# The second half's norm marked into the next product, and eight sums of squares made one, in a two-layer hybrid backbone

## The chip, the cores and the metric

The kernel runs on one core of one Trainium2 chip. The metric is the device time of one execution, in microseconds. Three runs of the kernel before stand behind its median.

## The reference, cut to what matters

A trunk of two layers works on 256 context tokens and 256 latent tokens of 1,024 channels, in float32. Each layer has three sub-layers: a half-step SwiGLU, a mixer (retention, a gated linear recurrence and attention, merged and projected), and a second half-step SwiGLU. Each of them begins with the same normalisation, and this is what the change touches:

```python
def _rms(x, g):
    xf = x.astype(jnp.float32)
    y = xf * lax.rsqrt(jnp.mean(xf * xf, axis=-1, keepdims=True) + NORM_EPS)
    return (y * g.astype(jnp.float32)).astype(x.dtype)

def _modulate(x, g, shift, scale):
    return _rms(x, g) * (1 + scale) + shift
...
x = x + m_l[:, 0..2] * sublayer(_modulate(x, norm_g, shift, scale))
```

Here `shift`, `scale` and the gate `m[:, 2]` are computed from the conditioning vectors, one set for context and one for latent tokens.

## The kernel before

**Layout.** The residual `x` stands in SBUF as eight tiles `x[d]` of 128 channels by 512 tokens: columns 0 to 255 are the context, 256 to 511 the latent tokens. The modulated input of a sub-layer is kept as two float32r tiles for each `d`, `hh[d]` (the rounded value) and `hl[d]` (the rest), and each weight likewise as `wh` and `wl`; a product is three matmuls, `wh*hh`, `wl*hh` and `wh*hl` (`mm3`, lines 145 to 147).

**The border between two sub-layers.** The last product of a sub-layer makes the eight output tiles of 128 channels one after the other. Six of them are made for all 512 tokens at once. The last two, `d` = 6 and 7, are made in `finish` in two halves: first columns 0 to 255 of both (tile `pl`), then columns 256 to 511 of both. A half is 72 matmuls of 256 columns behind a SwiGLU (two tiles of 12 contraction steps of three matmuls) and 48 behind the mixer of layer 0 (two tiles of 8 steps).

**What follows each half.** `update` adds the gated product to `x[d]` on VectorE (line 596), then `sumsq` squares it on ScalarE (line 585) and adds the square to `st["acc"]` on VectorE (line 587); the square of the last tile, `d` = 7, is not added but kept as `st["last"]`. `token_ms` lets TensorE sum over the channels: for each 128 tokens one matmul with `acc` and one with `last` as the weights and a single column of ones, into `ssq` (line 621). In float32 each of these is two instructions, so a half has eight. `rstd_bcast` makes the reciprocal root on VectorE (ten small instructions, `rv` and lines 161 to 169, then `dg`, line 609) and spreads it over the partitions with one matmul into `rb` (line 611). `modulate` then makes, for each of the eight `d`, `hn` on VectorE (line 641), `hh` on ScalarE (line 642) and `hl` on VectorE (line 643).

**The next product.** `proj_first` makes the first four tiles (`lx` ahead of the mixer, `pa` and `pb` ahead of a SwiGLU) with weights loaded ahead by `preload`. It goes by halves as well: for columns 0 to 255 first 64 matmuls with `hh` (item by item, for each of eight `k` the weights `wh` and `wl`, line 739), then 32 with `hl` (line 736); then the same 96 for columns 256 to 511.

**Where these stand.** `finish` runs with 512 tokens at four borders: layer 0 first SwiGLU to mixer, mixer to second SwiGLU, second SwiGLU to layer 1 first SwiGLU, and that to the mixer of layer 1. At the fifth border, inside layer 1, only latent tokens remain, and `finish_ahead` has an order of its own, written out by hand. `token_ms` is so called nine times.

**What sets the order.** Outside of the parts under `manual_schedule` a planner writes the order of each engine's instructions ahead of time: it follows the program on its own estimates of durations and gives each engine what it holds to be ready. The chip then runs each engine's list strictly in the order written. `issue_after(ins)` is a constraint on that order: what the block traces on the engine of `ins` is placed behind `ins`. `finish` uses it in this way: `marks` holds pairs of a count and an instruction, and a matmul step of the half that follows is held behind the instruction once the count is reached. With `MA, MB = 4, 13` the steps of the second half from number 4 on (12 matmuls) stand behind the first half's `ssq`, and those from number 13 on (39 matmuls) behind its `rb`. For the second half's own norm there is no such mark in the next product.

`hold` is the last `modulate` of the second half; weight splits (`wload`) and the background products of the conditioning (`pump`) that are traced after it are held behind it in the same way.

Of the kernel before, what the change touches and what calls it, by code (L numbers as in the profile page):

```python
# [16 lines left out]
P = 128  # L17
D = 1024
KD = D // P
# [15 lines left out]
SW = 128  # L35


MA, MB = 4, 13
NA, NB = 2, 4

LAG = 3
# [26 lines left out]
class Net:  # L68
# [509 lines left out]
    def sumsq(self, d, st, c0, c1):  # L578

        nc = self.nc  # L580
        sq = st["sq"][d] if d in st.setdefault("sq", {}) else self.tmp("sq")
        st["sq"][d] = sq
        if d == 0:
            st["acc"] = sq
        nc.scalar.activation(sq[:, c0:c1], self.x[d][:, c0:c1], AF.Square)
        if 0 < d < KD - 1:
            nc.vector.tensor_tensor(st["acc"][:, c0:c1], st["acc"][:, c0:c1], sq[:, c0:c1], op=ALU.add)
        if d == KD - 1:
            st["last"] = sq

    def update(self, d, ps, tab, c0, c1, st, nlo):

# [22 lines left out]
    def token_ms(self, st, c):  # L615

        nc = self.nc
        sp = self.sm_ps("ssq", [P, 2])
        for t in range(2):
            for n in ("acc", "last"):  # L620
                mm = nc.tensor.matmul(sp[:, t:t + 1], lhsT=st[n][:, c + t * P:c + (t + 1) * P],
                                      rhs=self.ones[:, 0:1], start=n == "acc", stop=n == "last")
        self.last_pe = mm.ins
        v = self.tiny("rv", [P, 2])
        nc.vector.tensor_scalar(v, sp, 1.0 / D, EPS, op0=ALU.mult, op1=ALU.add)
        return v
# [19 lines left out]
    def finish(self, tiles, tab, lo, st, nxt):  # L646


        nlo = nxt["lo"] if nxt else CTX
        if nxt:  # L650
            self.drain(nxt["tab"])
            self.h_tiles()
        ps = {d: self.mm_ps("pl") for d, _ in tiles}
        marks = []
        for c, v in self.halves(lo):
            n = 0
            for d, mms in tiles:
                for mm in mms(ps[d], c, c + 256):
                    with ExitStack() as es:
                        for at, ins in marks:  # L660
                            if n >= at:
                                es.enter_context(self.tc.issue_after(ins))
                        mm()
                    n += 1
                self.update(d, ps[d], tab, c, c + 256, st, nlo)
            if nxt and c >= nlo:
                v2 = self.token_ms(st, c)
                marks = [(MA, self.last_pe)]
                r = self.rstd_bcast(v2)
                marks += [(MB, self.last_pe)]  # L670
                self.hold = [self.modulate(d, r, nxt["tab"], c, v) for d in range(KD)][-1]

    def ahead_tiles(self, nxt):

        self.drain(nxt["tab"])
        self.xs = []
        for i in range(0, 2 * KD, 6):
            n = min(6, 2 * KD - i)
            t = self.big("xs", F32R, [P, n, TOK - CTX + 2])
            self.xs += [t[:, k] for k in range(n)]  # L680
            self.split(t[:, 0::2, 0:2], t[:, 1::2, 0:2], nxt["tab"]["Bt"][:, i // 2:(i + n) // 2])
# [45 lines left out]
    def proj_first(self, lo):  # L727

        pss = [self.mm_ps(name) for _, name in self.pre]
        mm = self.nc.tensor.matmul  # L730
        for sl in [slice(c, c + 256) for c, _ in self.halves(lo)]:
            for i in range(2):
                for ((wh, wl), _), ps in zip(self.pre, pss):
                    for k in range(KD):
                        if i:
                            mm(ps[:, sl], lhsT=wh[:, k], rhs=self.hl[k][:, sl], start=False, stop=k == KD - 1)
                            continue
                        for w in (wh, wl):
                            mm(ps[:, sl], lhsT=w[:, k], rhs=self.hh[k][:, sl], start=k == 0 and w is wh, stop=False)
        return pss  # L740
# [704 lines left out]
```

## Time and profile before

| what | value |
|---|---|
| median of three runs | 2136.7 us (2136.7 to 2139.08) |
| the profiled execution, its own time | 2137.75 us |
| its span, first to last instruction | 2135.9 us |
| mean granted TensorE clock | 0.999 |
| TensorE busy | 2099.5 us, 98% of the span |
| VectorE busy | 1526.1 us, 71% |
| ScalarE busy | 877.9 us, 41% |
| GpSimd busy | 29.2 us, 1% |

A busy TensorE isn't a TensorE at its peak: matmuls overlap, and their ends are modelled. What a matmul costs in a full stream is read from the distance of two starts, not from its duration. An idle engine that is not the one that sets the end costs nothing; here that engine is TensorE nearly everywhere, so that a change is worth what it does to the distances between TensorE's starts.

### The profile page before, as it was taken

Reading aid. Unit: us, or ns where it says so; the run is one execution under the profiler, and the core shown is the slowest. Engines: PE = TensorE matmul, PEld = TensorE weight load, DVE = VectorE, ACT = ScalarE, POOL = GpSimd, SP = SyncE. Lnnn points to the kernel's source line nnn. Section 1 sums busy time; section 2 is a strip of 40 time slices with the busy share of each in tenths; the row PEclk is TensorE's granted clock in tenths of the full one; section 3 lists DMA queues with packets and bytes.
Section 4 is the critical chain, followed back from the end, with each engine's and each line's share of the span. In section 5 each row is a group of like instructions: output and inputs, shape, how many; then the busy total and the mean of one; then the engine's idle time right before and its main releaser. Section 6 shows DMA issues by size and latency. Waiting matters only on the chain. (4 is left out here: it accounts for less than half of the span.)

```text
span 2135.9 us, 29550 instructions
## 1 busy us (share of the span) xinstructions
PE 2099.5 (98%) x11301; PEld 1788.5 (84%) x11301; DVE 1526.1 (71%) x2858; ACT 877.9 (41%) x1379; POOL 29.2 (1%) x48
## 2 busy tenths in 40 slices
PE   8999999999999999999999999999999999999998
PEld 5788888988878777988788898888889899989996
DVE  6998988675574866766766778777666777877555
ACT  4422323387323564332223332222233674665443
POOL 0000000100000000000000000000000000000001
PEclk9999999999999999999999999999999999999999
DMA  8566666332223314254654625465552435555663
GB/s 274 173 178 199 196 185 186 104 97 81 84 79 89 90 40 123 76 158 134 179 159 131 184 84 158 141 183 154 148 164 64 119 113 150 148 150 164 182 177 128
DMA packets 424239, 300.63 MB, mean 141 GB/s; under 512 B 11517, under 2 KB 372562, under 8 KB 424096
## 3 DMA queue, kind: packets, MB, share of 16 engines
q1 hardware_dynamic: 421120, 294.17, 47.0%
q0 software_dynamic: 1472, 3.42, 0.6%
q8 instruction: 89, 1.46, 0.3%
q10 hardware_dynamic: 1504, 1.13, 0.2%
q14 instruction: 54, 0.44, 0.1%
HBM read 297.64 MB, written 1.05 MB: 140 GB/s over the span
## 5 line engine op out<-in xcount | busy, mean ns | idle before, releaser
L132 ACT CAST wh<-raw 128x1024 fp32r<-128x1024 f32 (+3 forms) x437 | 412.5, 947 | 849.2 <-issue 187.3
L133 DVE TENSOR_TENSOR wl<-raw,wh 128x1024 fp32r<-128x1024 f32 (+3 forms) x437 | 476.0, 1092 | 248.2 <-ACT wh L132 244.3
L539 DVE SCALAR_TENSOR_TENSOR macc<-mraw,s_col,macc 128x512 f32<-128x512 f32 x448 | 315.9, 749 | 41.3 <-DMA mraw<-in_w_mod_dram 41.2
L145 PE MATMUL pb<-hh,wh 128*128 128x512 f32 (+1 forms) x656 | 238.8, 364 | 0.2 <-ACT wh L132 0.2
L147 PE MATMUL pb<-hh,wl 128*128 128x512 f32 (+1 forms) x656 | 238.6, 364 | 0.0
L146 PE MATMUL pb<-hl,wh 128*128 128x512 f32 (+1 forms) x656 | 238.4, 363 | 0.0
L147 PE MATMUL pa<-hh,wl 128*128 128x512 f32 (+1 forms) x624 | 226.1, 362 | 3.1 <-DVE wl L133 3.1
L145 PE MATMUL pa<-hh,wh 128*128 128x512 f32 (+1 forms) x624 | 226.1, 362 | 0.0
L146 PE MATMUL pa<-hl,wh 128*128 128x512 f32 (+1 forms) x624 | 225.8, 362 | 0.0
L145 PE MATMUL po<-g,wh 128*128 128x512 f32 x456 | 177.6, 390 | 1.1 <-ACT wh L132 1.1
L147 PE MATMUL po<-g,wl 128*128 128x512 f32 x456 | 177.9, 390 | 0.7 <-DVE wl L133 0.7
L146 PE MATMUL po<-g,wh 128*128 128x512 f32 x456 | 177.3, 389 | 0.0
L145 PEld LDWEIGHTS pb<-hh,wh 128*128 128x128 f32 x656 | 123.8, 189 | 19.9 <-ACT wh L132 0.6
L146 PEld LDWEIGHTS pb<-hl,wh 128*128 128x128 f32 x656 | 123.9, 189 | 19.6 <-DVE hl L643 0.3
L147 PEld LDWEIGHTS pb<-hh,wl 128*128 128x128 f32 x656 | 123.8, 189 | 19.6
L147 PEld LDWEIGHTS pa<-hh,wl 128*128 128x128 f32 x624 | 117.8, 189 | 22.2 <-DVE wl L133 3.9
L145 PE MATMUL gt<-hh,wh 128*128 128x512 f32 (+1 forms) x384 | 133.0, 346 | 0.1
L146 PEld LDWEIGHTS pa<-hl,wh 128*128 128x128 f32 x624 | 117.8, 189 | 18.0
L145 PEld LDWEIGHTS pa<-hh,wh 128*128 128x128 f32 x624 | 117.8, 189 | 17.8
L147 PE MATMUL gt<-hh,wl 128*128 128x512 f32 (+1 forms) x384 | 129.5, 337 | 0.2 <-DVE wl L133 0.2
L146 PE MATMUL gt<-hl,wh 128*128 128x512 f32 (+1 forms) x384 | 129.4, 337 | 0.0
L783 DVE TENSOR_TENSOR th<-th,pb 128x512 f32<-128x512 f32 (+1 forms) x86 | 53.7, 624 | 76.7 <-PE pb L147 73.4
(424 smaller groups left out, 4020.1 us busy)
## 6 DMA issues: line engine op xcount, KB each, us to landing
raw<-in_ffn_w_in_dram SPq DMA_DIRECT2D x176, 512.0 KB, 4.7
mraw<-in_w_mod_dram SPq DMA_DIRECT2D x132, 512.0 KB, 3.9
raw<-in_w_in_dram SPq DMA_DIRECT2D x108, 512.0 KB, 4.1
raw<-in_ffn_w_out_dram SPq DMA_DIRECT2D x48, 384.0 KB, 3.6
raw<-in_ffn_w_out_dram SPq DMA_DIRECT2D x48, 320.0 KB, 3.4
raw<-in_ffn_w_out_dram SPq DMA_DIRECT2D x22, 512.0 KB, 3.7
raw<-in_w_branch_dram SPq DMA_DIRECT2D x32, 256.0 KB, 2.8
raw<-in_w_out_dram SPq DMA_DIRECT2D x16, 512.0 KB, 5.3
```

The lines of the kernel that those rows point to most:

```text
L132: nc.scalar.copy(wh[:, :nk * n], raw[:, :nk * n])
L133: nc.vector.tensor_tensor(wl[:, :nk * n], raw[:, :nk * n], wh[:, :nk * n].bitcast(F32), op=ALU.subtract)
L145: mm(out, lhsT=ah, rhs=bh, start=first, stop=False)
L146: mm(out, lhsT=ah, rhs=bl, start=False, stop=False)
L147: mm(out, lhsT=al, rhs=bh, start=False, stop=last)
L539: nc.vector.scalar_tensor_tensor(acc, raw[:, k], sc, acc, op0=ALU.mult, op1=ALU.add)
L783: nc.vector.tensor_tensor(th[:, lo:], th[:, lo:], pb[:, lo:], op=ALU.mult)
```

## The change

The last square is added to `acc` on VectorE like the others, and `token_ms` has one matmul in place of two for each 128 tokens. The marks of the first half's norm go from steps 4 and 13 to steps 5 and 14 (15 and 42 matmuls). The second half's norm gets two marks of its own in `proj_first`: its matmuls from number 15 on stand behind the second half's `ssq`, those from number 51 on behind its `rb`. They hold for matmuls counted in the order in which they are traced, so that ahead of `ssq` only the first 15 of the first item may stand.

```diff
-MA, MB = 4, 13
+MA, MB = 5, 14
+LA, LB = 5, 17
...
         nc.scalar.activation(sq[:, c0:c1], self.x[d][:, c0:c1], AF.Square)
-        if 0 < d < KD - 1:
+        if d:
             nc.vector.tensor_tensor(st["acc"][:, c0:c1], st["acc"][:, c0:c1], sq[:, c0:c1], op=ALU.add)
-        if d == KD - 1:
-            st["last"] = sq
...
         for t in range(2):
-            for n in ("acc", "last"):
-                mm = nc.tensor.matmul(sp[:, t:t + 1], lhsT=st[n][:, c + t * P:c + (t + 1) * P],
-                                      rhs=self.ones[:, 0:1], start=n == "acc", stop=n == "last")
+            mm = nc.tensor.matmul(sp[:, t:t + 1], lhsT=st["acc"][:, c + t * P:c + (t + 1) * P],
+                                  rhs=self.ones[:, 0:1], start=True, stop=True)
...
                 self.hold = [self.modulate(d, r, nxt["tab"], c, v) for d in range(KD)][-1]
+        self.marks = [(3 * at, ins) for (_, ins), at in zip(marks, (LA, LB))]
...
         pss = [self.mm_ps(name) for _, name in self.pre]
-        mm = self.nc.tensor.matmul
+        n = 0
+
+        def mm(*args, **kw):
+            nonlocal n
+            with ExitStack() as es:
+                for at, ins in self.marks:
+                    if n >= at:
+                        es.enter_context(self.tc.issue_after(ins))
+                self.nc.tensor.matmul(*args, **kw)
+            n += 1
+
```

## Rows read from the trace of the kernel before

**Rows 1.** Waits of TensorE, whole run: total us, times, longest us.

```profile
PE lx L739 <- ACT hh L642: 2.2, 2, 1.1
...
PE pa L739 <- ACT hh L642: 1.6, 2, 1.1
```

**Rows 2.** TensorE's instructions on the tile ssq: duration in ns min/median/max.

```profile
L621 PE MATMUL ssq<-ones,sq x72: 164/250/250, 390.5 to 1938.2; 128*128 128x1 f32 x72
```

**Rows 3.** Timeline of TensorE, first border: start, duration, line, tile, count.

```profile
392.19 0.73 PE L621 MATMUL ssq<-ones,sq 128*128 128x1 f32 x6
...
396.09 0.59 PE L611 MATMUL rb<-dg,ones 128*128 128x256 f32 x2
396.33 0.47 PE L145 MATMUL pl<-g,wh 128*128 128x256 f32 x1
...
400.48 2.68 PE L739 MATMUL lx<-hh,whl 128*128 128x256 f32 x21
403.00 0.28 PE L621 MATMUL ssq<-ones,sq 128*128 128x1 f32 x2
...
406.94 0.73 PE L621 MATMUL ssq<-ones,sq 128*128 128x1 f32 x6
...
412.89 0.59 PE L611 MATMUL rb<-dg,ones 128*128 128x256 f32 x2
414.60 1.58 PE L739 MATMUL lx<-hh,whl 128*128 128x256 f32 x11 [1.12 <-ACT hh L642]
```

**Rows 4.** Timeline of VectorE, first border.

```profile
392.95 0.16 DVE L625 TENSOR_SCALAR rv<-ssq 128x2 f32<-128x2 f32 x1 [1.74 <-PE ssq L621]
...
394.92 0.48 DVE L609 TENSOR_SCALAR dg<-cst,rs_y 128x128 f32<-128x128 f32 x2
...
396.72 3.22 DVE L641 SCALAR_TENSOR_TENSOR hn<-x,mod_o,rb 128x256 f32<-128x256 f32 x8 [0.31 <-PE rb L611]
399.86 0.42 DVE L587 TENSOR_TENSOR sq<-sq 128x256 f32<-128x256 f32 x1
400.20 2.86 DVE L643 SCALAR_TENSOR_TENSOR hl<-hn,mod_o,hh 128x256 fp32r<-128x256 f32 x7
402.97 0.48 DVE L596 SCALAR_TENSOR_TENSOR x<-pl,mod_o,x 128x256 f32<-128x256 f32 x1
```

**Rows 5.** Timeline of ScalarE, first border.

```profile
391.24 0.42 ACT L585 ACTIVATE sq<-x 128x256 f32<-128x256 f32 x1 [3.32 <-DVE x L596]
...
403.48 0.42 ACT L585 ACTIVATE sq<-x 128x256 f32<-128x256 f32 x1 [2.92 <-DVE x L596]
```

**Rows 6.** Timeline of TensorE, second border (mixer to SwiGLU, layer 0).

```profile
880.38 0.95 PE L621 MATMUL ssq<-ones,sq 128*128 128x1 f32 x8
...
884.75 0.70 PE L611 MATMUL rb<-dg,ones 128*128 128x256 f32 x2
...
886.56 0.50 PE L739 MATMUL pa<-hh,whl 128*128 128x256 f32 x2
...
899.96 0.50 PE L739 MATMUL pa<-hh,whl 128*128 128x256 f32 x2 [0.53 <-ACT hh L642]
```

**Rows 7.** Timeline of VectorE, second border.

```profile
885.49 3.22 DVE L641 SCALAR_TENSOR_TENSOR hn<-x,mod_o,rb 128x256 f32<-128x256 f32 x8 [0.79 <-PE rb L611]
888.62 0.48 DVE L596 SCALAR_TENSOR_TENSOR x<-pl,mod_o,x 128x256 f32<-128x256 f32 x1
889.02 3.25 DVE L643 SCALAR_TENSOR_TENSOR hl<-hn,mod_o,hh 128x256 fp32r<-128x256 f32 x8
```

**Rows 8.** Timeline of ScalarE, second border.

```profile
879.97 0.42 ACT L585 ACTIVATE sq<-x 128x256 f32<-128x256 f32 x1
...
889.22 0.40 ACT L585 ACTIVATE sq<-x 128x256 f32<-128x256 f32 x1
```

**Rows 9.** Stretches near the end: length, busy by engine, granted TensorE clock, DMA.

```profile
2126.00:2128.00 2.00, 0.46 (x3) 0.03 (x1) 1.86 (x9) 0.02 (x1) 0.56 (x1) 1.00 0.00 0
...
2130.00:2131.00 1.00, 0.00 (x0) 0.00 (x0) 0.83 (x6) 0.00 (x0) 0.01 (x1) 0.51 0.98 365
```

## The prediction, as put on record

> **What bounds the kernel now.** I read the busy times of the page first, then who TensorE waits for over the whole run, then the order of each engine at the four borders. TensorE is busy 98% of the span, so only three things can move the time: its instruction count, its waits, and the order in which it meets them. Its waits on the tiles that the change is about are small: 2.2 us on `lx` and 1.6 us on `pa`, four waits in all, one for each border of 512 tokens [rows 1].
>
> The first border shows how such a wait comes about. TensorE starts the next product at 400.48 and puts out 21 matmuls until 403.00, which is 0.12 us for each [rows 3]. The second half's `ssq` follows at 403.00 and 406.94, its `rb` only at 412.89, behind all 96 matmuls of the first half. The next matmul needs the second half's `hh` and starts at 414.60, 1.71 us later [rows 3]. An unhindered start comes 0.24 us after `rb` [rows 3]; of the other 1.47 us the trace books 1.12 as waiting. I count 1.3 us lost. Borders 3 and 4 repeat this to 0.02 us; border 2 waits 0.53 us [rows 6].
>
> VectorE tells the rest, and it is what decides my forecast. The last `pl` matmul of the second half is issued just ahead of 400.48, but the update of `x[7]` that needs it starts at 402.97 [rows 4]. VectorE isn't waiting then: it works off the first half's `modulate`, eight `hn` from 396.72, one addition of squares, seven `hl` [rows 4]. So in the kernel before the second half's norm is late by 2.5 us at its first step, and TensorE doesn't feel it, since it has 96 matmuls in hand.
>
> **The change part by part.**
>
> *Fewer `ssq` instructions.* There are 72 of them, 8 for each of nine halves [rows 2]; 36 go. A group of six lasts 0.73 us and a group of two 0.28 [rows 3], so one costs 0.11 us and a half saves 0.44 us. Nine halves: 4.0 us, if nothing else waits.
>
> *The eighth square on VectorE.* One more 128x256 addition, 0.42 us [rows 4], now lies between the square and `ssq`. In the first half of borders 1, 3 and 4 it is hidden: the square ends at 391.66 [rows 5], the addition at 392.1, and the mark, three matmuls later and without the 0.2 us of the early pair, comes at about 392.32 instead of 392.19. VectorE is idle there, 1.74 us ahead of `rv` [rows 4]. `rb` has room as well: `rv` to the end of `dg` is 392.95 to 395.40 [rows 4], and `rb` stood at 396.09 [rows 3]. If that cover went, each late 0.1 us would be TensorE's own.
>
> *The first half's marks.* They move `rb` three matmuls, 0.36 us, closer to the end of `pl`: from `rb` to the product it is now 4.39 us (396.09 to 400.48), then 4.03. The four saved instructions lie ahead of both.
>
> *The second half's marks.* With them `rb` no longer stands behind 96 matmuls: 45 remain behind it, 5.4 us, where `rb` to the first `hh` needs 1.71 [rows 3]. The 1.3 us go. But the 16th matmul now stands behind `ssq`, so behind it are queued 81 of the 96 matmuls, and everything after them; they wait for whatever `ssq` waits for. What is late is `x[7]`. From `rb` to its update took 6.88 us [rows 3, 4]. The product's end of `pl` comes 0.36 us sooner against `rb`; at border 2 it came 2.7 us sooner (884.75 to 886.56 against 4.39) [rows 6], and there the update stands seven places earlier, ahead of all `hl` [rows 7]. So a place is some 0.38 us, and I take one place: 6.48 us. Then the square, 0.51 us later and 0.42 long [rows 4, 5], ends at 7.41. The two `hl` left end at 7.68 (0.40 each), the new addition at 8.1, `ssq` can start at 8.15 after `rb`, which is 4.1 us after the product's start. The 15 matmuls are out after 1.8 us. TensorE stands still for 2.3 us.
>
> Borders 1, 3 and 4: minus 1.3 for the old wait, minus 0.88 for two halves of `ssq`, plus 2.3: +0.1 us each, +0.4 in all. `rb` after `ssq` costs no further wait: it needs 2.5 us [rows 4], and 36 matmuls give 4.3.
>
> *Border 2.* Its half has 48 matmuls, so after `rb` only 6 remain (9 before). In the first half the square is late (879.97, behind ScalarE's conditioning copies) [rows 8]; the addition ends near 880.95, the mark comes at 880.74, and the `rb` chain also slips by 0.2 us, so that the saved 0.44 us is spent: `rb` near 884.9 against 884.75 [rows 6]. Now `x[7]` is ahead of the `hl`, but its square stands behind eight `hh` on ScalarE, at 889.22 [rows 8], and the new addition comes ready when all `hl` are already queued, 889.02 to 892.27 [rows 7]. All slips by 0.15, so the addition ends at 892.85. The 15 matmuls of one item have only the `hh` to follow and end by 889.7. From 892.9: 0.44 for `ssq`, 36 matmuls 4.3, `rb` 0.43, 45 matmuls 5.4, so the second half starts at 903.4 against 899.96 [rows 6]: +3.5 us. If the addition slips in right behind its square, it is +1.0; this is the lower bound.
>
> *The fifth border* has only the saving, -0.44; its order is written by hand, and I see nothing late. If the addition came late there, at most its 0.42 would be lost.
>
> Sum: 0.4 + 3.5 - 0.4 = +3.5 us. The profiled execution took 2137.75 (span 2135.9 and 1.85 around it), 1.05 above the median; the sum goes onto the median: 2140.2 us. Bounds: a stall of nothing at all borders gives -1.3*3 - 0.6 - 4.0 = -8.5; `x[7]` behind all `hl` and border 2 in full gives +5.
>
> *A rule on the clock.* Near the end of this trace TensorE is through with its last matmuls around 2126.5, and at 2130 its granted clock is 0.51, that is 1.2 GHz in place of 2.4 [rows 9]; in this trace's four waits at the borders it stayed at 1.0. The Trainium skill ("TensorE: Matmul & The Clock Gate", Part 1) says that an idle TensorE falls to half its clock until it has been busy again. By that rule the matmuls behind border 2's long wait would run at half speed and the time would be about 2145 (worked out below); by the rows of the borders, 2140.2. The trace agrees on the fall, and no row shows it inside the kernel.
>
> **The rivals.** *The marks do what they say* (faster): the update, the square and the addition get in ahead of the first half's `hl`. The product's start then lies 0.2 us past the last `hn`, the square ends behind the last `hh` about 0.85 us after it, `ssq` at 1.4, inside 1.8. Each long border gains 1.3 + 0.88, border 2 still loses 1.0, the fifth gains 0.4: -6 us, 2130.7. For it: at border 2 the update does stand ahead of the `hl`. Against it: at the long borders it ended behind seven.
>
> *The update falls behind the last `hl`* (slower): then `ssq` comes 0.58 us later at each long border, +1.7, 2141.9. It decides from 0.8 us more than my sum, which is 0.3 us a border. For it: only one `hl` is behind it now. Against: the 0.36 us.
>
> *The clock falls at border 2* (slower): its stall of 3.2 us is not much shorter than the idle stretch at the end behind which the clock stands at half [rows 9]. 81 matmuls at twice 0.12 us cost at most 9.7 us; half of that gives 2145.
>
> *The stalls are there but milder* (border 2 at its lower bound): 2137.7.
>
> **How the numbers follow.** About 0.2%, 4.3 us, is what a measurement of this kernel can tell from no change. My forecast, 2140.2 (its own range 2138 to 2142): 0.50, of it 0.36 within 0.2% and 0.14 above. Marks as meant: 0.18, faster. Update behind all `hl`: 0.19, 0.15 slower and 0.04 same. Milder: 0.07, same. Clock: 0.06, slower. Faster 0.18, same 0.47, slower 0.35. The range has to take in the faster case and the first slower one: 2130.5 to 2144.
>
> **What would show it.** Right: at each border `lx` or `pa` in a run of 15, a gap of about 2.3 us (border 2: over 3) released by the addition, 4 `ssq`, 36 matmuls, `rb`, 45, and no wait at the second half's start; 36 `ssq` in all. Wrong: no gap ahead of `ssq`, `x[7]` updated before the `hl`; a granted clock of 0.5 behind a border; or other waits of TensorE, far from the borders, moved by the new order.

## The result, and the profile after

The changed kernel is slower: 2148.61 us as the median of six executions (2146.4 to 2154.09), against 2136.98 for the kernel before beside it (2136.34 to 2139.08). The ratio is 1.0054, with a 95% interval of 1.0044 to 1.0064, so 11.6 us more where 3.5 were forecast, and above the range. The profiled execution is the shortest of the six, 2146.4 us with a span of 2144.6: 8.7 us above the span before.

The stall that was forecast is there. TensorE's waits over the whole run (total us, times, longest us) and the `ssq` instructions, against [rows 1, 2]:

```profile
PE ssq L620 <- DVE sq L589: 9.7, 4, 3.0
```

```profile
L620 PE MATMUL ssq<-ones,sq x36: 168/250/352, 392.7 to 1946.9; 128*128 128x1 f32 x36
```

The waits of `lx` and `pa` for `hh` [rows 1] are gone from the second halves, 36 `ssq` instructions are left of 72 [rows 2], and four waits of 9.7 us in all stand ahead of the second halves' `ssq`. At the first border, TensorE's timeline (start, duration, line, tile, count), against [rows 3]:

```profile
396.34 0.59 PE L611 MATMUL rb<-dg,ones 128*128 128x256 f32 x2
...
400.37 1.96 PE L738 MATMUL lx<-hh,whl 128*128 128x256 f32 x15
404.57 0.58 PE L620 MATMUL ssq<-ones,sq 128*128 128x1 f32 x4 [2.25 <-DVE sq L589]
405.01 1.21 PE L738 MATMUL lx<-hh,whl 128*128 128x256 f32 x8
...
405.81 5.26 PE L738 MATMUL lx<-hh,whl 128*128 128x256 f32 x30
410.91 0.59 PE L611 MATMUL rb<-dg,ones 128*128 128x256 f32 x2
411.15 1.91 PE L738 MATMUL lx<-hh,whl 128*128 128x256 f32 x13
```

VectorE at the same place, against [rows 4]:

```profile
400.45 2.46 DVE L642 SCALAR_TENSOR_TENSOR hl<-hn,mod_o,hh 128x256 fp32r<-128x256 f32 x6
402.82 0.48 DVE L596 SCALAR_TENSOR_TENSOR x<-pl,mod_o,x 128x256 f32<-128x256 f32 x1
403.22 0.87 DVE L642 SCALAR_TENSOR_TENSOR hl<-hn,mod_o,hh 128x256 fp32r<-128x256 f32 x2
404.01 0.42 DVE L589 TENSOR_TENSOR sq<-sq 128x256 f32<-128x256 f32 x1
```

Fifteen matmuls, then nothing for 2.25 us, because VectorE makes six `hl` of the first half, then the update of `x[7]`, then two more `hl`, then the new addition. That is the order and nearly the time that the prediction has. What it does not have is the row of 405.81: 30 matmuls take 5.10 us until `rb`, 0.17 each and not 0.12. (The rows of 405.01 and 405.81 come from two windows and share two matmuls; between `ssq` and `rb` there are 36.) At the third border, the same view:

```profile
1263.32 1.96 PE L738 MATMUL pa<-hh,whl 128*128 128x256 f32 x15
1267.53 0.58 PE L620 MATMUL ssq<-ones,sq 128*128 128x1 f32 x4 [2.25 <-DVE sq L589]
...
1272.37 0.59 PE L611 MATMUL rb<-dg,ones 128*128 128x256 f32 x2
```

The stall is the same, but from `ssq` to `rb` it is 4.84 us here and 6.34 at the first border. The windows say why (length; busy time of PE, PEld, DVE, ACT and POOL, each with the number of instructions that reach into the window; granted TensorE clock, DMA share, GB/s):

```profile
405.00:406.00 1.00, 1.00 (x10) 1.00 (x10) 0.67 (x5) 0.00 (x0) 0.00 (x0) 1.00 0.00 0
407.00:408.00 1.00, 1.00 (x6) 1.00 (x6) 0.61 (x3) 0.00 (x0) 0.00 (x0) 0.50 0.00 0
...
410.00:411.00 1.00, 1.00 (x10) 1.00 (x10) 0.00 (x0) 0.00 (x0) 0.00 (x0) 1.00 0.00 0
896.00:898.00 2.00, 2.00 (x11) 2.00 (x11) 1.40 (x9) 0.00 (x0) 0.00 (x0) 0.50 0.00 0
1268.00:1270.00 2.00, 2.00 (x18) 2.00 (x19) 1.54 (x10) 0.00 (x0) 0.54 (x1) 1.00 0.21 57
1636.00:1638.00 2.00, 2.00 (x12) 2.00 (x11) 1.05 (x6) 0.00 (x0) 0.00 (x0) 0.50 0.00 0
```

Behind the stalls of borders 1, 2 and 4 the granted clock is 0.5, the lower of the two levels (1.2 GHz), for some microseconds, and in these windows TensorE is busy all the time: 11 or 12 matmuls reach into 2 us in place of 18. Border 3 keeps 1.00. Busy time alone hides this: the page has TensorE at 98% as before.

The second border, on TensorE, VectorE and ScalarE, against [rows 6 to 8]:

```profile
889.11 3.19 PE L738 MATMUL pa<-hh,whl 128*128 128x256 f32 x15 [0.40 <-ACT hh L641]
895.30 0.98 PE L620 MATMUL ssq<-ones,sq 128*128 128x1 f32 x4 [3.00 <-DVE sq L589]
...
902.25 0.59 PE L611 MATMUL rb<-dg,ones 128*128 128x256 f32 x2
```

```profile
891.18 0.48 DVE L596 SCALAR_TENSOR_TENSOR x<-pl,mod_o,x 128x256 f32<-128x256 f32 x1
891.57 3.25 DVE L642 SCALAR_TENSOR_TENSOR hl<-hn,mod_o,hh 128x256 fp32r<-128x256 f32 x8
894.74 0.42 DVE L589 TENSOR_TENSOR sq<-sq 128x256 f32<-128x256 f32 x1
```

```profile
891.76 0.40 ACT L587 ACTIVATE sq<-x 128x256 f32<-128x256 f32 x1
```

The square is ready at 892.16, and the addition that needs it comes behind all eight `hl`, 2.6 us later.

For the account I take one length at each border from TensorE's timeline: from the first `hh` matmul of the next product to the first matmul behind its 192. It holds the stall, the second half's `ssq` and `rb`, and the old wait, but not the first half's `ssq` and `rb`.

| kernel | lengths at borders 1 to 4, us | stall ahead of ssq, us | clock of 0.5 behind it |
|---|---|---|---|
| before | 25.74, 25.02, 25.73, 25.72 | none | none |
| after | 27.88, 30.96, 26.39, 27.88 | 2.25, 3.00, 2.25, 2.24 | 1, 2, 4 |
| e5, after again | 27.86, 30.87, 27.89, 27.87 | 2.25, 3.01, 2.25, 2.25 | all four |
| e1, fifteen useless matmuls | 26.37, 28.38, 26.39, 26.38 | 0.44, 1.21, 0.44, 0.44 | none |
| e2, marks at 36 and 66 | 23.90, 27.32, 23.91, 23.90 | 0, 1.62, 0, 0 | 2 |
| e7, marks at 24 and 57 | 25.32, 28.78, 25.31, 25.30 | 1.17, 2.89, 1.17, 1.17 | 2 |
| e6, marks without the addition | 25.90, 25.57, 27.40, 25.91 | 1.29, 0, 1.29, 1.29 | 3 |
| e4, first half's hl deferred | 23.92, 25.84, 23.92, 23.92 | 0, 0.47, 0, 0 | none |
| e8, the same, marks at 21 and 57 | 23.91, 25.12, 23.91, 23.91 | 0, 0.35, 0, 0 | none |
| e9, e4 with VectorE made late | 29.52, 31.10, 28.27, 28.18 | 2.54, 3.23, 2.54, 2.54 | all four |
| e3, one ssq matmul, no marks | 25.28, 25.44, 25.27, 25.28 | none | none |
| e10, each ssq matmul twice | 26.62, 25.89, 26.62, 26.61 | none | none |
| e13, last square left out | 23.91, 23.74, 23.91, 23.90 | none | none |
| e14, addition alone | 25.72, 25.91, 25.72, 25.73 | none | none |

After less before is +2.14, +5.94, +0.66 and +2.16, together +10.9 us. The rest of the run is 2.2 us shorter, which makes the 8.7 us between the two spans. That is not the saving in `ssq`: 2.1 of the 2.2 us are shorter waits of TensorE for weights between borders 2 and 4, and against the other profile of the kernel before (e12) the same rest is 2.9 us longer.

### The profile page after: what moved, and what is told of

It reads as the page before. It is cut to its first block, busy times and chain, and to the rows that moved or that the text cites. A ratio compares the mean times of both kernels' runs of the same rounds, so it can differ in the third digit from the quotient of the medians.

```text
span 2144.6 us, 29489 instructions
## 1 busy us (share of the span) xinstructions
PE 2101.3 (98%) x11265; PEld 1790.3 (83%) x11265; DVE 1530.6 (71%) x2867; ACT 876.6 (41%) x1379; POOL 29.2 (1%) x48
## 5 line engine op out<-in xcount | busy, mean ns | idle before, releaser
L149 PEld LDWEIGHTS pb<-hh,wl 128*128 128x128 f32 x656 | 123.9, 189 | 19.5
```

Source lines behind the costliest of these rows:

```text
L149: mm(out, lhsT=al, rhs=bh, start=False, stop=last)
```

## The experiments

My theory: VectorE's queue makes the second half's `ssq` late (the stalls, some 5 us dearer than before in these lengths), and TensorE's half clock behind the stalls doubles the damage. The rivals: the stalls alone, or the new order of instructions. The runs e1 to e4, e5 to e8, e9 to e12, and e13 with e14 each shared a chip and the runs of the kernel before on it; ratios are to those. The edits of e1 to e4, e7, e8 and e11 are made on the changed kernel, that of e9 on e4, and those of e6, e10, e13 and e14 on the kernel before; of the longer ones only the lines that matter are shown.

**e1: the stall filled with useless work.** The first 15 matmuls of the next product are made twice, into the same tile.

```diff
+        (wh, wl), _ = self.pre[0]
+        for i in range(15):
+            self.nc.tensor.matmul(pss[0][:, 0:256], lhsT=(wh, wl)[i % 2][:, i // 2], rhs=self.hh[i // 2][:, 0:256],
+                                  start=i == 0, stop=i == 14)
```

> The 15 matmuls ahead of the second half's ssq are made twice at each of the four borders (the second pass starts the sums anew, so the result is the same): 60 useless matmuls, some 7 us of TensorE work. Theory A (the stall ahead of ssq sends TensorE to half its clock, and that is most of what the forecast missed): the waits ahead of ssq shrink from 2.25 us to about 0.4 at three borders and from 3.0 to about 1.2 at the second, the granted clock stays at 1.0 there, and the kernel, with more work, gets faster than the changed one by 5 us or more: about 2140 to 2143 us. Rival B (the time is lost in waiting alone, or in an order that the new constraints spoil elsewhere): the useless work only takes the place of waiting, and the time stays at 2148 us or rises.

Measured: 2140.07 us, ratio 1.0033 (1.0021 to 1.0044), with 60 matmuls more than the changed kernel. At the second border:

```profile
886.87 3.19 PE L743 MATMUL pa<-hh,whl 128*128 128x256 f32 x15 [0.41 <-ACT hh L641]
889.89 1.96 PE L738 MATMUL pa<-hh,whl 128*128 128x256 f32 x15
893.06 0.58 PE L620 MATMUL ssq<-ones,sq 128*128 128x1 f32 x4 [1.21 <-DVE sq L589]
...
897.90 0.59 PE L611 MATMUL rb<-dg,ones 128*128 128x256 f32 x2
```

`ssq` stands 6.19 us behind the product's start, exactly as in the changed kernel (889.11 to 895.30), but from `ssq` to `rb` it is 4.84 us and not 6.95. VectorE's lateness is all there; only most of the idle time is gone, and the half clock with it:

```profile
894.00:896.00 2.00, 2.00 (x19) 2.00 (x19) 1.69 (x11) 0.00 (x0) 0.00 (x0) 1.00 0.00 0
```

So this row of the table is the price of the lateness at full clock, +0.63, +3.36, +0.66 and +0.66, 5.3 us together, and what the changed kernel has above it, 1.51, 2.58, 0 and 1.50, is the half clock: 5.6 us.

**e2: later marks.** `LA, LB` of 12 and 22: 36 matmuls ahead of `ssq` and 66 ahead of `rb`.

```diff
-LA, LB = 5, 17
+LA, LB = 12, 22
```

> The marks in the next product go from 15 and 51 matmuls to 36 and 66; all else is as in the changed kernel. Theory A: ssq is ready 4.1 us, that is 34 matmuls, after the product's start at borders 1, 3 and 4, so the wait there goes to nothing, at the second border a wait below 1 us is left; no half clock; the old wait at the second half's start stays away too, since 30 matmuls (3.6 us) remain behind rb, which needs 1.7. Time about 2131 us, 0.3% below the kernel before. Rival B (the order that the marks force is bad as such, or other waits moved): still slower than before, 2140 us or more.

Measured: 2132.59 us, ratio 0.9994 (0.9985 to 1.0002): no change from before. No stall at borders 1, 3 and 4; border 2 still waits 1.62 us, where I had expected less than 1, and runs at half clock behind it.

**e3: the one-matmul sum alone.** The marks in the next product are left out.

```diff
-        self.marks = [(3 * at, ins) for (_, ins), at in zip(marks, (LA, LB))]
+        self.marks = []
```

> Only the sums of squares and the first half's marks are changed, no marks in the next product: the planner places the second half's ssq and rb itself, late, as before. Theory A: 36 instructions of ssq fewer, 4 us, and the old wait of 1.1 us at the second half's start stays at three borders; 2133 us, 0.2% below before; no half clock. Rival B (the longer chain through VectorE costs as well): 2137 us or more, with waits ahead of the first half's ssq.

Measured: 2133.58 us, ratio 1.0000 (0.9991 to 1.0008). The old waits are back, 1.1 us at all four borders (0.5 at border 2 before), and no clock falls. So it takes the marks to make the loss. But the 4 us for 36 instructions are not there either; e10 to e14 go after that.

**e4: the first half's `hl` deferred.** They are issued behind the second half's `dg`, so that nothing stands between the update of `x[7]`, its square and the addition.

```diff
...
+                if c:
+                    with self.tc.issue_after(self.last_dg):
+                        for rest in late:
+                            rest()
...
```

> The marks stay at 15 and 51, but the first half's eight hl are queued behind the second half's dg on VectorE, so that the update of x[7], its square and its addition have only the hn and hh ahead of them. Theory A with its step on VectorE's queue: x[7] is updated about 0.2 us after the product's start instead of 2.5, ssq is ready after 1.4 us, before the 15 matmuls are out: no wait at borders 1, 3 and 4, about 0.5 us at the second, no half clock; 2131 us, 0.3% below before. If the stall had another cause than the queue on VectorE, it would stay at 2.3 us and the time at 2148.

Measured: 2129.9 us, ratio 0.9984 (0.9975 to 0.9993), below both kernels. Its first border on TensorE and VectorE:

```profile
400.13 1.97 PE L745 MATMUL lx<-hh,whl 128*128 128x256 f32 x15
401.94 0.51 PE L620 MATMUL ssq<-ones,sq 128*128 128x1 f32 x4
...
406.71 0.59 PE L611 MATMUL rb<-dg,ones 128*128 128x256 f32 x2
```

```profile
399.88 0.41 DVE L589 TENSOR_TENSOR sq<-sq 128x256 f32<-128x256 f32 x1
400.33 0.48 DVE L596 SCALAR_TENSOR_TENSOR x<-pl,mod_o,x 128x256 f32<-128x256 f32 x1
401.30 0.42 DVE L589 TENSOR_TENSOR sq<-sq 128x256 f32<-128x256 f32 x1 [0.48 <-ACT sq L587]
```

With the same marks, `ssq` now comes 1.81 us after the product's start and waits for nothing. What made it late at borders 1, 3 and 4 was the first half's `hl` in VectorE's order and nothing else. At border 2 a wait of 0.47 us is left: there the square stands behind eight `hh` on ScalarE until 887.62, 2.66 us after the product's start, and VectorE waits for it.

**e5: the changed kernel again**, beside three relatives.

> The changed kernel as it is, beside three relatives on one chip. Theory A (the second half's ssq stands still for VectorE and TensorE's clock stands at half behind the stall in most executions): stalls of 2.25 us at borders 1, 3, 4 and 3.0 at border 2, windows with a granted clock of 0.5 behind two to four of them, not always the same ones; ratio 1.0045 to 1.006, and among its executions the longer ones show the lower mean clock. Theory B (the stalls alone, half clock by chance in one profile): ratio 1.001 to 1.002, and no half clock at the borders this time.

Measured: 2148.3 us, ratio 1.0059 (1.0046 to 1.0072). The stalls are those of the table to 0.01 us, and now border 3 falls as well:

```profile
1268.00:1270.00 2.00, 2.00 (x15) 2.00 (x15) 1.63 (x10) 0.00 (x0) 0.54 (x1) 0.75 0.23 68
1270.00:1272.00 2.00, 2.00 (x11) 2.00 (x11) 0.48 (x2) 0.00 (x0) 0.00 (x0) 0.50 0.02 6
```

So one and the same stall is followed by half clock in one execution and not in another. This shows its price without any edit: border 3 is 26.39 us long with the stall of 2.25 at full clock, the same as in e1, and 27.89 at half clock. In the first set of six, the two with the lowest mean clock (0.993) are the longest, 2150.43 and 2154.09 us.

**e6: the marks without the addition.** The last square stays apart, as before, with eight `ssq` instructions.

The first half's marks are those of before as well.

```diff
 MA, MB = 4, 13
+LA, LB = 5, 17
...
+        self.marks = [(3 * at, ins) for (_, ins), at in zip(marks, (LA, LB))]
...
```

> The marks in the next product (matmuls 15 and 51) with the last square kept apart as before: eight ssq instructions, and the second half's ssq waits for the square of x[7] and not for an addition behind it. The addition goes from the late chain: 0.45 to 0.5 us less stall, 1.7 to 1.8 us at borders 1, 3, 4, and at border 2, where the square is ready 3 us ahead of the addition, 0 to 0.5. Theory A (clock): with border 2's stall its half clock goes as well, some 3 us less of lost clock there; against that 36 ssq instructions more at 0.11, +4.0; ratio 1.002 to 1.005, so less than the changed kernel beside it although it has 36 instructions more. Theory B (stalls alone): -1.4 and -3.0 of stall against +4.0, within 1 us of the changed kernel.

Measured: 2139.02 us, ratio 1.0020 (1.0011 to 1.0029): 36 instructions more than the changed kernel, and 0.39% of the time less. The waits are shorter than I expected, since the two instructions on `acc` leave ahead of the one wait:

```profile
PE ssq L623 <- ACT sq L587: 3.9, 3, 1.3
```

Half clock only behind border 3 (1260 to 1264).

**e7: marks at 24 and 57 matmuls.**

```diff
-LA, LB = 5, 17
+LA, LB = 8, 19
```

> The second half's marks at matmuls 24 and 57 in place of 15 and 51: nine more matmuls ahead of ssq, 1.1 us of cover. Stalls of 1.1 to 1.2 us at borders 1, 3, 4 (half of the changed kernel's), 2 to 3 at border 2. Theory A, if any stall halves the clock: 1.7 us of lost clock at most borders still, ratio 1.002 to 1.004. Theory A, if a stall of 1.2 us is survived at full clock (as the 1.1 us wait at the second half's start was in the kernel before): half clock behind border 2 alone, ratio 0.999 to 1.002.

Measured: 2138.84 us, ratio 1.0015 (1.0006 to 1.0024). Three stalls of 1.17 us with the clock at 1.00 behind them, one of 2.89 with half clock. The second of the two forecasts.

**e8: e4 with marks at 21 and 57 matmuls** (`LA, LB = 7, 19`).

> The first half's eight hl queued behind the second half's dg on VectorE, and the second half's marks at matmuls 21 and 57 in place of 15 and 51: 0.7 us more cover ahead of ssq. It should take the 0.47 us that were left at border 2 and nothing else: no wait ahead of ssq at any border, clock 1.0 at all of them, 0 to 1 us below the version with the marks at 15 and 51, ratio 0.997 to 0.999. Rival: with marks this late rb and hh come later as well, and a wait at the second half's start returns: ratio 0.999 or above.

Measured: 2133.94 us, ratio 0.9986 (0.9977 to 0.9995). I had expected no wait at all; border 2's went from 0.47 only to 0.35 us. Its length is 0.7 us shorter than in e4, too little for the ratio to tell.

**e9: e4 with VectorE made late.** Six operations that change nothing stand between the second half's last addition and its `ssq`.

```diff
+        if d == KD - 1 and getattr(self, "slow", False):
+            for _ in range(6):
+                nc.vector.tensor_tensor(st["acc"][:, c0:c1], st["acc"][:, c0:c1], st["acc"][:, c0:c1], op=ALU.max)
...
+                self.slow = c and nxt and nlo == 0
```

> The version with the first half's eight hl put behind the second half's dg, which had no wait ahead of ssq at borders 1, 3 and 4 (0.47 us at border 2) and a ratio of 0.9984, with six useless operations of 128x256 (acc = max(acc, acc), 0.42 us each) between the second half's last addition and its ssq at the four borders: VectorE late by 2.5 us, TensorE's order the same. Stalls of 2.3 us at borders 1, 3, 4 and 3.0 at border 2 should come back. Theory A (what costs is the stall and the half clock behind it, whatever makes ssq late): half clock behind two to four of the stalls, 9.4 us of stall and 4 to 7 us of lost clock above that version, ratio 1.0045 to 1.006. Theory B (the stalls alone): 9.4 us, ratio 1.0025 to 1.003 with full clock. Rival C (the loss of the changed kernel lies in its order of instructions and not in the stalls): ratio below 1.001.

Measured: 2146.26 us, ratio 1.0057 (1.0044 to 1.0069).

```profile
PE ssq L623 <- DVE sq L592: 10.9, 4, 3.2
```

```profile
403.89 0.98 PE L623 MATMUL ssq<-ones,sq 128*128 128x1 f32 x4 [2.54 <-DVE sq L592]
404.74 6.76 PE L750 MATMUL lx<-hh,whl 128*128 128x256 f32 x34
411.33 0.59 PE L614 MATMUL rb<-dg,ones 128*128 128x256 f32 x2
```

```profile
404.00:406.00 2.00, 2.00 (x10) 2.00 (x11) 0.91 (x6) 0.00 (x0) 0.00 (x0) 0.50 0.00 0
```

From `ssq` to `rb` it is 7.44 us, in e4 4.77. The lengths are 19.5 us above e4's. Of these, 10.8 are the later `ssq` (10.4 of them booked as stall), and the other 8.6 are the half clock, which stands behind all four stalls. The best version becomes as slow as the changed kernel, with `ssq` at the place in TensorE's order that it has in e4, by the stalls and the clock behind them. This settles it against the rival of the order, and against the stalls without the clock, which would have given 1.0025 to 1.003.

**e10: each `ssq` matmul twice**, in the kernel before.

```diff
-            for n in ("acc", "last"):
+            for n in ("acc", "last") * 2:
```

> The kernel before with each ssq matmul made twice into the same place: 72 instructions more in nine halves. If an ssq instruction costs TensorE 0.11 us, as the groups of six say, +8 us, ratio 1.0035 to 1.004, and the 4 us for 36 fewer was a right price that something else ate in the run without marks. If they lie in gaps or in the slack of weight transfers: ratio below 1.002, and the 4 us were never there to gain.

Measured: 2140.69 us, ratio 1.0033 (1.0021 to 1.0045), 7.0 us for 72 instructions; in the table 0.87 to 0.89 us for the eight of a half. An `ssq` instruction costs 0.11 us, as [rows 3] said.

**e11: e3 with the first half's marks as before** (`MA, MB = 4, 13`).

> The last square added to the others, one matmul in place of two, no marks in the next product, and the first half's marks left at steps 4 and 13 as before. The run with steps 5 and 14 showed a ratio of 1.000 where 36 instructions fewer should give 0.998. If the later first-half marks had cost what the instructions saved: ratio 0.998. If not: again 0.9995 to 1.0005, and a new wait is to be seen at the first half's ssq, where the addition is 0.4 us later against a mark 0.36 us earlier.

Measured: 2134.26 us, ratio 1.0003 (0.9994 to 1.0012), and the lengths of e3 within 0.02 us. The new wait that I expected at the first half's `ssq` is there, 0.45 us at border 2 and 0.14 at border 4. The first half's marks are not what ate the saving.

**e12: the kernel before, one execution** on e11's chip.

> The kernel before, unchanged, for a profile on the same chip as its relatives: full clock at all four borders, waits of 1.1 us (border 2: 0.5) at the second half's start, 72 ssq instructions; the stretches between the borders, to be laid beside those of the version without marks, show whether the time of TensorE's waits for weights differs between two executions of one kernel by as much as the 4 us looked for.

Measured: 2132.67 us. The lengths are those of before within 0.02 us and the clock is 1.00 at all borders. Its wait of `pa` for a weight near 1053 is 0.63 us, where the first profile of the same kernel has 2.37: single profiles differ by microseconds for that alone. Outside of the four lengths the two profiles of the kernel before differ by 5.0 us.

**e13 and e14: the two parts of the one-matmul sum, each alone**, in the kernel before. e13 leaves the last square's matmul out, so that its norm covers seven of the eight tiles; e14 adds the square and keeps its matmul, so that it counts twice.

```diff
# e13
-            for n in ("acc", "last"):
+            for n in ("acc",):
# e14
-        if 0 < d < KD - 1:
+        if d:
```

> The kernel before with the ssq matmul of the last square left out and no addition in its place: the sum of squares covers seven of the eight tiles, so the norm is another. 36 ssq instructions fewer, nothing else on any engine. If 36 fewer are worth what 72 more cost (0.11 us each in the products' lengths), -4.0 us less what waits for the same things as before: ratio 0.998 to 0.999. If TensorE's time elsewhere takes it back whatever VectorE does: ratio 0.9995 to 1.0005.

> The kernel before with the last square added to the others on VectorE and its own ssq matmul kept as well: it is counted twice, so the norm is another. All 72 ssq instructions, nine additions of 0.42 us more on VectorE, each ahead of an ssq. If the additions are hidden, as the prediction has it for the first halves: ratio 0.9995 to 1.0005, and then they don't explain where the 4 us of the one-matmul versions went. If the addition costs TensorE its 0.42 us at each half: +3 to +4 us, ratio 1.0015 to 1.002, and it has eaten the saving.

Measured: e13 2131.26 us, ratio 0.9969 (0.9959 to 0.9979), so -6.6 us; e14 2140.12, ratio 1.0011 (1.0003 to 1.002), so +2.4 us. e13 gained more than the instructions, since its second half's norm no longer needs `x[7]`: no wait for `hh` is left. Its lengths are 6.75 us shorter than before's, of which about 1.8 (four times 0.44) are the `ssq` instructions and about 5.0 the old wait. From the measured -6.6 that leaves some -1.6 us for all 36 instructions, with 2.1 us of uncertainty. e14 lies between its two forecasts and shows that with the first half's marks at 4 and 13 the addition isn't hidden: border 2's second half waits 1.11 us for `hh` in place of 0.53 (its length is 0.89 us above before's), and its first half's `ssq` stands still for 0.45 us behind VectorE. -1.6 and +2.4 together are the nothing of e3 and e11 within what was measured. Some 1 us of e14's 2.4 has no row of its own at the borders, and the first halves' share of the saving didn't reach the medians; where these lie stays open in the main.

## Why the prediction was wrong

*Fewer `ssq` instructions, -4.0.* The price of one was right (e10). In the second halves, 1.8 of the 4.0 us, the saving is in the lengths, and in the first halves of borders 1, 3 and 4 the addition is hidden as forecast: the profile after has no wait ahead of `ssq` or `rb` there, and 0.09 and 0.11 us at border 2. But the 1.8 us that the sum has outside of the products, three first halves and the fifth border, do not show against single profiles that differ by 5.0 us there. Some 55 us ahead of the fifth border TensorE even has a new wait, 1.08 us (1.00 in e5) of `ptp` for ScalarE near 1892 us, which neither profile of the kernel before has; its cause stays open. Without the marks the whole term came to nothing (e3 and e11: 1.0000 and 1.0003), so there it was mis-sized by some 4 us.

*The old wait goes, -1.3 at a border.* Right: no wait at any second half's start.

*The new stall, 2.3 us.* Right: 2.25, 2.25 and 2.24. The update of `x[7]` was forecast 6.48 us after `rb` and starts at 402.82, 6.48 after 396.34; the place in the queue, behind six `hl`, is also the one taken. On the way there the prediction misread border 2: the product's start came 2.58 us sooner against `rb` (4.39 less 1.81), not 2.7; a place is then 0.37 us, and the count of one place stays. The rival with the update behind the last `hl` and the one with the marks as meant are both out.

*Border 2, +3.5, with a stall of 3.2.* The stall is 3.00; at full clock e1 has +3.36. Right, and the milder case is out.

*The clock.* This is the step that failed. The prediction put the fall at border 2 alone, gave it 0.06, and had for the others only that the clock stayed at 1.0 in four waits of before; but those were of 1.12 and 0.53 us, and the stalls it forecast were twice that and more. It applied the fall to the longest stall alone, though the other three are some three quarters as long. The lower clock followed three of the four stalls in one profile, four in the next (e5), and cost 5.6 and 7.0 us. For the three long borders the sum had +0.1 us each; with the clock they cost 1.5 more where it fell. At border 2 it cost 2.6 and 2.5 us, where the rival had put half of 9.7.

With it the account closes. The products' lengths were forecast 5.2 us longer (0.56 at three borders and 3.5), e1 has 5.3 at full clock, and the half clock adds 5.6 in the first profile and 7.0 in e5's: 10.9 and 12.3. The medians of the two sets lie 11.6 and 12.1 us above the kernel before, which leaves little room for the 1.8 us to be saved elsewhere. That is no proof, since only these two executions have a profile: how often the clock fell in the others isn't shown, and their mean clocks, 0.993 to 0.997, say no more than that it differs.

The trace agrees with the rule of the Trainium skill ("TensorE: Matmul & The Clock Gate", Part 1) that an idle TensorE falls to half its clock until it has been busy again. It does so in 12 of the 13 stalls of 2.24 us or more. The table of the two states in that part of the Trainium skill puts the fall behind a longer idle stretch than any of these, so here the measurement decides. Nothing in the runs fixes how short a stall can be: 1.62 us was followed by half clock the one time it occurred (e2), 1.29 once in three (e6), 1.17 not in three (e7).

## What to carry to other kernels

A stall of TensorE has two prices, its own length and what the following work takes at half clock; write both terms for every stall in the forecast, not for the longest alone, and read the granted clock behind it, since the busy share shows nothing. A mark that moves a dependent instruction forward on one engine is worth only what the engine that feeds it can do by then: read that engine's strict order first, and move what stands in its way (e4), before or in place of the mark. And a saving on the critical engine that is paid for with an addition on another should be tried in its two parts (e13, e14): here each part moved the time by a few microseconds, and both together by nothing that could be measured.

## What the runs showed of the hardware

- The lower clock followed stalls of 2.24 to 3.23 us in 12 of 13 cases (after, e5, e7, e9), and none of the ones of 1.21 us or less; the same stall of 2.25 us at border 3 was followed by it in one execution and not in another.
- At half clock TensorE shows as busy all the time, while 11 or 12 matmuls reach into 2 us in place of 18 or 19 (after at 896 and 1636, e1 at 894).
- Useless matmuls in the place of idle time made the kernel faster than without them: 2140.07 us with 60 more (1.0033) against 1.0054 and 1.0059.
- Eight of the sixteen profiles (e1, e2, e4, e7, e8, e9, e13, e14) show a clock of 0.5 in some windows between 14 and 26 us from the start, far from all that was changed, among them the fastest real version. In the three where it lasts longest (e2, e7, e8) the product at the first border starts at 402.6 to 403.8 us, in the eight without it at 399.2 to 400.6. That is as much as the effects that were looked for, so that only medians over many executions could tell them.
